# Three tile rings instead of one in the retention stage, and sums of squares over both heads of a pair at once

## The chip, the cores and the metric

The kernel runs on one core of a Trainium2 chip. The metric is the device time of one execution in microseconds (us). The core has a matrix engine (TensorE, PE in the profile; its weight loads are PEld), three engines for elementwise work (VectorE = DVE, ScalarE = ACT, GpSimd = POOL) and SyncE (SP), whose queue issues most of the DMA transfers. Each engine runs its own instructions strictly in order. An instruction that must wait holds up everything behind it on its engine.

## The reference, cut to what matters

One layer of a streaming encoder on a sequence of 2048 tokens, width 1024: a normalised input is projected to 7168 columns, which feed a chunked attention branch (8 heads), a retention branch (8 heads, key size 64, value size 128) and gates; the two branches are projected back, gated, merged, projected once more and normalised. The part that the change touches is the retention branch and its norm by head:

```python
s = jnp.einsum('bnqhd,bnkhd->bnhqk', qc, kc) * intra_decay
o_intra = jnp.einsum('bnhqk,bnkhe->bnqhe', s, vc)
...
state = state * chunk_decay[None, :, None, None] + kv_n        # from chunk to chunk
o_cross = jnp.einsum('bnqhd,nbhde->bnqhe', qc, state_prev) * cross_decay.T[:, :, None]
o = (o_intra + o_cross).astype(jnp.float32).reshape(B, S, H, dv)
mean = jnp.mean(o, axis=-1, keepdims=True)
var = jnp.mean(jnp.square(o - mean), axis=-1, keepdims=True)
o = (o - mean) * lax.rsqrt(var + GN_EPS)
o = o.reshape(B, S, H * dv) * gn_gain.astype(jnp.float32)
branch_r = jnp.einsum('bsf,fd->bsd', o_r * jax.nn.silu(g_r), w_out_ret[l])
```

## The kernel before, in words

Every float32 matrix operand is split into a high and a low part, and products are made of three matmuls (high by high, high by low, low by high). The large products ("dense work": jobs `p0`, `g0`, `p1`, `g1`, `ba`, `br`, `out`, tiles named `ps_...`, `wh_...`, `wl_...`) are one long stream of steps of three to six matmuls. The two halves of the sequence (s = 0 and 1) each go through an attention stage and a retention stage, and there the dense stream fills the time between the stage's own matmuls: `fill(n)` (L683) emits some n steps of it. Work that must come a little later is put off by a number of steps with `later` (L245), stores with `put` (L258). So the order on every engine is fixed in the program text; almost all of it is recorded through one helper, which is why nearly every row of the profile has line L143.

**Retention** (L1612) works on 16 units in each half: pairs of heads p = 0 to 3, and for each pair four steps `st` of 256 tokens. In unit (p, st) it does for each head i = 0, 1 of the pair:

- `scores`: four matmuls into a PSUM tile `sr`; then DVE multiplies by the decay mask (`sm <- sr, dm`, 128x384), ACT rounds that to its high part (`sh <- sm`), POOL makes the low part (`sl <- sm, sh`).
- `output`: matmuls into one half of the PSUM tile `o`, of which there is only one (`bufs=1`): first the state times q (`o <- qr, sstk`), then `sh` and `sl` with the values `vr`.

After the second head, `evacuate`: ACT copies `o` to `oz` (stored to DRAM as `ors`) and squares it to `o2`, then splits `o2` into `o2h` (ACT) and `o2l` (POOL). One unit later, `sums` lets PE add up the squares over the 128 value rows: a matmul with a one-hot column matrix `ohr` puts the sum into one row of the PSUM tile `ssq`. At the end of a stage a chain of 12 DVE operations makes 1/sqrt of it, which is stored as `rsscr`; much later `finish_yr` (L1237) loads a row of it, broadcast over the partitions, as `rb`.

Loads of a unit: `kr` (2 DMAs), `qr` for head 0 and head 1 (2 DMAs each), issued two units ahead; `kd` and two `vr`, issued one unit ahead; two masks `dm` for each pair. All of them go through SP's queue, together with the stores.

All of these tiles, loads, masks, scores, outputs and squares alike, come from **one ring** `E` of 22 buffers of 128x512 floats (2 KB a partition). The layer that builds the program gives a tile whichever buffer of its ring is free at that point of the order. The first instruction that writes the tile then waits until the buffer's previous tile has been read for the last time: by a matmul, by an elementwise operation, or, for a tile that is stored, until the store has landed.

Of the kernel before, what the change touches and what calls it, by code (L numbers as in the profile page):

```python
# [11 lines left out]
F32 = mybir.dt.float32  # L12
F32R = mybir.dt.float32r
# [8 lines left out]
P = 128  # L22
# [6 lines left out]
B = 512  # L29
NB = SEQ // B  # L30
T = 256
# [22 lines left out]
CS = 6  # L54
E_PROJ = 19
E_ATT = 11
E_RET = 22
E_MRG = 23
PR_BUFS = 5
ATT_FILLS = (1.0, 1.0)  # L60
# [9 lines left out]
ONE = 31  # L70
# [3 lines left out]
def hybrid_kernel(  # L74
# [28 lines left out]
    epool, xpool = [None], [None]  # L103
# [10 lines left out]
    def E(name, dt=F32, shape=(P, 512)):  # L114
        return epool[0].tile(list(shape), dt, tag="e", name=name)
# [37 lines left out]
    pe, act, dve, pool = Ordered(nc.tensor), Sometimes(nc.scalar), Sometimes(nc.vector), Sometimes(nc.gpsimd)  # L153
    dma = Ordered(nc.sync).dma_start
# [9 lines left out]
    ohr = const.tile([P, NOH], F32R, name="ohr")  # L164
# [1072 lines left out]
    def finish_yr(h, b, m, lead, hold=0):  # L1237

        a, u, r = (E(f"{n}_{h}_{b}") for n in ("yr", "yv", "rb"))
        dma(a, orscr[h // 2][b][h % 2])  # L1240
        dma(u, urscr[h][b])
        dma(r, rsscr[b // 2][8 * b + h].rearrange("(o d) -> o d", o=1).broadcast_to([P, B]))

        def gated():
            dve.scalar_tensor_tensor(a, a, gn[:, h:h + 1], u, ALU.mult, ALU.mult)

        later(lead, gated)
        later(lead + 2, lambda: (pool if m is None else dve).tensor_tensor(a, a, r, ALU.mult))
        if m is None:
            put(lead + 8, yrscr[h], a)  # L1250
            return
        wh, wl = (w[:, h % 4, :] for w in R[m])
        at = max(lead + 5, hold - steps[0])
        later(at, lambda: act.copy(wh, a))
        later(at + 2, lambda: dve.tensor_tensor(wl, a, r32(wh), ALU.subtract))
# [356 lines left out]
    def retention(s, ps_ret):  # L1612
# [43 lines left out]
        def load_state(p, st):  # L1656

            if st == 4:
# [2 lines left out]
                dma(r32(sstk).rearrange("p i c -> p (i c)"), r32(skscr[p]))  # L1661
                sstks[p, 4] = sstk

        def load_mask(p, i):
            dms.setdefault(p, []).append(E(f"dm_{p}_{i}")[:, 0:T + P])
            dma(dms[p][i], dmask[2 * p + i])

        def scores(p, st, i):

            nm = f"{p}_{st}_{i}"  # L1670
            ks, qs = tiles[p, st]
            sp = ps_ret.tile([P, 512], F32, tag="sr", bufs=2, name=f"sr_{nm}")[:, 0:T + P]
            for kk in range(2):
                o = sp[:, kk * T:T + kk * P]
                kcol = ks[:, i, kk * P:(kk + 1) * P]
                pe.matmul(o, kcol, qs[i][:, 0, kk * P:], start=True, stop=False)
                pe.matmul(o, kcol, qs[i][:, 1, kk * P:], start=False, stop=True)
            got = []

            def masked():  # L1680
                sm = E(f"sm_{nm}")[:, 0:T + P]
                dve.tensor_tensor(sm, sp, dms[p][i], ALU.mult)
                later(2, lambda: high(sm))

            def high(sm):
                got.append(E(f"sh_{nm}", F32R)[:, 0:T + P])
                act.copy(got[0], sm)
                later(2, lambda: low(sm))

            def low(sm):  # L1690
                got.append(E(f"sl_{nm}", F32R)[:, 0:T + P])
                pool.tensor_tensor(got[1], sm, r32(got[0]), ALU.subtract)

            later(1, masked)
            return got
# [63 lines left out]
        def evacuate(p, st, ops):  # L1759
            b, un = st // 2, st % 2  # L1760
            nm = f"{p}_{st}"
            got = []

            def out_():
                oz = E(f"oz_{nm}")
                o2 = E(f"o2_{nm}")
                act.copy(oz, ops)
                act.activation(o2, ops, AF.Square)
                put(
                    2,  # L1770
                    orscr[p][b][:, :, un * T:(un + 1) * T].rearrange("i p t -> p i t"),
                    oz.rearrange("p (i t) -> p i t", i=2),
                )
                later(2, lambda: high(o2))

            def high(o2):
                got.append(E(f"o2h_{nm}", F32R))
                act.copy(got[0], o2)
                later(2, lambda: low(o2))

            def low(o2):
                got.append(E(f"o2l_{nm}", F32R))
                pool.tensor_tensor(got[1], o2, r32(got[0]), ALU.subtract)

            later(1, out_)

            def sums():
                sure(lambda: len(got) == 2)
                for i in range(2):
                    r = 8 * b + 2 * p + i  # L1790
                    for n, t in enumerate(got):
                        pe.matmul(
                            ssq[:, un * T:(un + 1) * T], ohr[:, ONE - r:ONE - r + 32],
                            t[:, i * T:(i + 1) * T],
                            start=not begun[0], stop=(p == 3 and st == 4 * s + 3 and i == 1 and n == 1),
                            skip_group_check=True,
                        )
                        begun[0] = True

            return sums  # L1800

# [240 lines left out]
```

## Time and profile before

| | |
|---|---|
| Time, median of three runs | 1909.71 us (1906.38, 1909.71, 1910.21) |
| The profiled execution | 1909.69 us, of which its span, first to last instruction, is 1907.9 us |
| PE busy over the span | 1866.9 us (98%) |
| Retention of half 0 (566 to 735 us) | 169.0 us, PE busy 161.80 us, DMA engines 88% busy |
| Retention of half 1 (1313 to 1497 us) | 184.0 us, PE busy 180.40 us, DMA engines 91% busy |

In the quoted views, a row of the waits is "who waited <- for whom: us in total, times, longest us"; a row of the timeline is "start us, length us, engine, line, operation, out<-in, count, [idle time of the engine before it <- what ended it]"; a row of the windows is "from:to, length, busy us (x instructions) of PE, PEld, DVE, ACT, POOL, then granted TensorE clock, busy share of the DMA engines, GB/s". The median time of the three runs and the profiled execution agree to 0.02 us.

### The profile page before, as it was taken

The page shows a single profiled execution, that of the slowest core. Times are in us where ns is not written, and L with a number is a line of the kernel's source. Part 1 is how long each engine was busy: PE and PEld are TensorE (multiplying, and loading weights), DVE is VectorE, ACT ScalarE, POOL GpSimd, SP SyncE. Part 2 cuts the span into 40 slices and gives each one's busy share as a digit, 9 for nine tenths or more (in the row PEclk, how much of TensorE's full clock was granted, in tenths as well). Part 3 has the DMA queues.
Part 4 walks back from the last instruction along what each step waited for, and adds up shares of the span by engine and source line. Part 5 has one row for each costly group of instructions (what it writes and reads, how often), then busy time and mean ns, then how long its engine had stood idle before and what let it go on. Part 6 is the DMA issues. An engine that isn't in the chain of part 4 may idle for free. (4 is left out here: it accounts for less than half of the span.)

```text
span 1907.9 us, 31062 instructions
## 1 busy us (share of the span) xinstructions
PE 1866.9 (98%) x10213; PEld 1604.4 (84%) x10213; DVE 1355.7 (71%) x2456; ACT 933.1 (49%) x1931; POOL 665.3 (35%) x583
## 2 busy tenths in 40 slices
PE   7999999999999999999999999999999999999998
PEld 6899889888888888899889888887888878888886
DVE  6879888677655658889798677765546766767665
ACT  7555554666654455443333666664455321223544
POOL 0102105455645561001105554554564000002775
PEclk9999999999999999999999999999999999999999
DMA  6586976666549987775776656555998999986673
GB/s 197 158 275 200 282 265 213 185 193 185 175 144 278 279 257 258 231 233 195 222 247 202 185 165 180 166 150 155 275 283 265 326 355 345 322 291 227 209 238 127
DMA packets 325553, 435.88 MB, mean 228 GB/s; under 512 B 29880, under 2 KB 191184, under 8 KB 325392
## 3 DMA queue, kind: packets, MB, share of 16 engines
q1 hardware_dynamic: 260096, 368.35, 60.7%
q10 hardware_dynamic: 65296, 65.55, 11.2%
q8 instruction: 81, 1.33, 0.3%
q14 instruction: 80, 0.66, 0.1%
HBM read 288.14 MB, written 145.64 MB: 227 GB/s over the span
## 5 line engine op out<-in xcount | busy, mean ns | idle before, releaser
L143 POOL TENSOR_SCALAR pr<-pr,rsum 128x640 f32<-128x640 f32 (+4 forms) x128 | 100.0, 781 | 197.7 <-DVE rsum L143 130.7
L143 DVE TENSOR_TENSOR ptl<-tp,pth 128x512 fp32r<-128x512 f32 (+1 forms) x168 | 100.3, 597 | 91.7 <-ACT pth L143 77.8
L143 ACT ACTIVATE pr<-pr,mn 128x640 f32<-128x640 f32 (+4 forms) x128 | 97.9, 765 | 123.3 <-DVE mn L143 97.3
L143 PE MATMUL ps_g_x<-r,wh_g 128*128 128x512 f32 x448 | 141.5, 397 | 1.0 <-ACT u_g L143 0.9
L143 PE MATMUL ps_g_z<-r,wh_g 128*128 128x512 f32 x448 | 141.1, 396 | 0.0
L143 POOL TENSOR_TENSOR l_vr<-vrt,h_vr 128x512 fp32r<-128x512 f32 x32 | 47.7, 1492 | 202.4 <-DMA qrs<-l_q 131.6
L143 POOL TENSOR_TENSOR t_out<-raw_out 128x512 f32<-128x512 f32 x7 | 14.1, 2008 | 263.2 <-DVE wl_out L143 263.2
L143 DVE CUSTOM_DVE_ANT_0 pr<-wide,bt 128x640 f32<-128x640 f32 (+4 forms) x128 | 93.7, 732 | 16.5 <-PE wide L143 13.5
L143 ACT CAST pth<-tp 128x512 fp32r<-128x512 f32 (+1 forms) x168 | 85.3, 507 | 38.9 <-PE tp L143 34.2
L143 PE MATMUL wide<-ka,qa 128*128 128x384 f32 (+1 forms) x448 | 94.9, 327 | 2.9 <-DVE mn L143 2.7
L143 DVE TENSOR_TENSOR sm<-sr,dm 128x384 f32<-128x384 f32 x64 | 35.6, 556 | 85.3 <-PE sr L143 33.9
L143 ACT CAST wh_p<-raw_p 128x512 fp32r<-128x512 f32 x111 | 67.9, 618 | 51.0 <-PE ps_p_y L143 18.2
L143 POOL TENSOR_TENSOR sl<-sm,sh 128x384 fp32r<-128x384 f32 x64 | 69.8, 1090 | 64.8 <-ACT sh L143 44.0
L143 PEld LDWEIGHTS tp<-ident,pr 128*128 128x128 f32 x560 | 71.8, 141 | 23.5 <-POOL pr L143 1.0
L143 PEld LDWEIGHTS ps_g_x<-r,wh_g 128*128 128x128 f32 x448 | 79.6, 189 | 13.9 <-ACT u_g L143 2.3
L143 PEld LDWEIGHTS ps_g_z<-r,wh_g 128*128 128x128 f32 x448 | 79.5, 188 | 12.4
L143 PE MATMUL tp<-ident,pr 128*128 128x128 f32 x560 | 89.0, 272 | 0.3
L143 PE MATMUL ps_g_z<-r,wl_g 128*128 128x512 f32 x224 | 88.2, 394 | 0.0
L143 PE MATMUL ps_g_x<-r,wl_g 128*128 128x512 f32 x224 | 88.1, 393 | 0.0
L143 POOL TENSOR_TENSOR wl_g<-t_g,wh_g 128x512 fp32r<-128x512 f32 x56 | 75.5, 1349 | 35.1 <-ACT wh_g L143 33.8
L143 DVE TENSOR_TENSOR wl_p<-raw_p,wh_p 128x512 fp32r<-128x512 f32 x111 | 79.5, 723 | 7.7 <-ACT wh_p L143 5.4
L143 POOL TENSOR_TENSOR t_g<-raw_g,t_g 128x512 f32<-128x512 f32 x56 | 73.8, 1318 | 28.1 <-issue 8.9
(927 smaller groups left out, 6016.7 us busy)
## 6 DMA issues: line engine op xcount, KB each, us to landing
raw_g<-in_w_in_dram ACTq DMA_DIRECT2D x56, 512.0 KB, 4.9
raw_p<-in_w_in_dram ACTq DMA_DIRECT2D x50, 512.0 KB, 5.8
qa<-qas SPq DMA_DIRECT2D x128, 128.0 KB, 3.4
qr<-qrs SPq DMA_DIRECT2D x128, 128.0 KB, 4.8
vr<-vrs SPq DMA_DIRECT2D x64, 256.0 KB, 5.6
ka<-kas SPq DMA_DIRECT2D x56, 256.0 KB, 4.1
va<-vas SPq DMA_DIRECT2D x40, 256.0 KB, 3.4
kds<-kdt_k SPq DMA_DIRECT2D x32, 256.0 KB, 4.8
```

What stands on the lines that cost most here:

```text
L143: return tc.keep_in_program_order(op(*a, **k))
```

## The change

The ring of 22 becomes three rings, 11 buffers `e` of 2 KB for the loads (`kr`, `qr`, `kd`, `vr`) and the four tiles of the closing DVE chain, 9 buffers `d` of 1.5 KB for masks and scores (`dm`, `sm`, `sh`, `sl`, which only ever use 384 columns), and 4 buffers `o` of 2 KB for `oz`, `o2`, `o2h`, `o2l`. That is 24 buffers instead of 22 in 0.5 KB a partition less. The sums of squares of a unit are made by two matmuls over 512 columns (both heads at once) instead of four over 256. A unit then has one row of `ssq` (row 4 st + p, head and token along it) where it had two half rows, and the load of `rb` collects its row from two pieces of 256 floats.

```diff
-E_RET = 22
+E_RET = 11
+D_RET = 9
+O_RET = 4
...
         dma(a, orscr[h // 2][b][h % 2])
         dma(u, urscr[h][b])
-        dma(r, rsscr[b // 2][8 * b + h].rearrange("(o d) -> o d", o=1).broadcast_to([P, B]))
+        by_head = rsscr[b // 2].rearrange("(b u p) (i t) -> b p i u t", u=2, p=4, i=2)
+        dma(
+            r.rearrange("p (u t) -> p u t", u=2),
+            by_head[b, h // 2, h % 2].rearrange("(o u) t -> o u t", o=1).broadcast_to([P, 2, T]),
+        )
...
+        def D_(name, dt=F32):
+            return epool[0].tile([P, T + P], dt, tag="d", bufs=D_RET, name=name)
+
+        def O_(name, dt=F32):
+            return epool[0].tile([P, 512], dt, tag="o", bufs=O_RET, name=name)
+
         def load_mask(p, i):
-            dms.setdefault(p, []).append(E(f"dm_{p}_{i}")[:, 0:T + P])
+            dms.setdefault(p, []).append(D_(f"dm_{p}_{i}"))
             dma(dms[p][i], dmask[2 * p + i])
...
             def masked():
-                sm = E(f"sm_{nm}")[:, 0:T + P]
+                sm = D_(f"sm_{nm}")
...
-                got.append(E(f"sh_{nm}", F32R)[:, 0:T + P])
+                got.append(D_(f"sh_{nm}", F32R))
...
-                got.append(E(f"sl_{nm}", F32R)[:, 0:T + P])
+                got.append(D_(f"sl_{nm}", F32R))
...
             def out_():
-                oz = E(f"oz_{nm}")
-                o2 = E(f"o2_{nm}")
+                oz = O_(f"oz_{nm}")
+                o2 = O_(f"o2_{nm}")
...
-                got.append(E(f"o2h_{nm}", F32R))
+                got.append(O_(f"o2h_{nm}", F32R))
...
-                got.append(E(f"o2l_{nm}", F32R))
+                got.append(O_(f"o2l_{nm}", F32R))
...
             def sums():
                 sure(lambda: len(got) == 2)
-                for i in range(2):
-                    r = 8 * b + 2 * p + i
-                    for n, t in enumerate(got):
-                        pe.matmul(
-                            ssq[:, un * T:(un + 1) * T], ohr[:, ONE - r:ONE - r + 32],
-                            t[:, i * T:(i + 1) * T],
-                            start=not begun[0], stop=(p == 3 and st == 4 * s + 3 and i == 1 and n == 1),
-                            skip_group_check=True,
-                        )
-                        begun[0] = True
+                r = 4 * st + p
+                for n, t in enumerate(got):
+                    pe.matmul(
+                        ssq, ohr[:, ONE - r:ONE - r + 32], t, start=not begun[0],
+                        stop=(p == 3 and st == 4 * s + 3 and n == 1), skip_group_check=True,
+                    )
+                    begun[0] = True
```

No instruction changes its place on any engine; only the 64 matmuls fall away. What moves are the waits. In the rows below a tile's name is followed by its pair, its step, where it has one its head, and a running number; in brackets stands whom the instruction waits for (DMAHW... is the landing of a DMA).

On ACT, in the first retention stage around unit (3, 1), the rows before:

```order
L143 CAST sh_3_1_1_8790<-sm_3_1_1_8766 128x384 [waits DVE_49]
L143 ACTIVATE u2_g0_11_8410<-u2_g0_11_8410 128x512 [waits DVE_49]
L143 CAST wh_g0_12_2_8804<-t3_g0_12_8689 128x512 [waits PE_49]
L143 CAST sstk_3_1_8797<-state_7087 64x256 [waits DMAHW6_49]
L143 CAST sh_3_2_0_8847<-sm_3_2_0_8837 128x384 [waits DMAHW4_49,DVE_49]
L143 COPY u2_g0_12_8853<-ps_g0_12_x_8807 128x512 [waits PE_49]
L143 CAST wh_g0_12_4_8856<-t1_g0_12_8494 128x512
L143 COPY oz_3_1_8884<-o_3_1_8774 128x512 [waits PE_49,Pool_49]
L143 ACTIVATE o2_3_1_8885<-o_3_1_8774 128x512
```

and the same instructions in the changed kernel:

```order
L145 CAST sh_3_1_1_8766<-sm_3_1_1_8742 128x384 [waits DVE_49]
L145 ACTIVATE u2_g0_11_8392<-u2_g0_11_8392 128x512 [waits DVE_49]
L145 CAST wh_g0_12_2_8780<-t3_g0_12_8667 128x512 [waits PE_49]
L145 CAST sstk_3_1_8773<-state_7087 64x256 [waits DMAHW6_49]
L145 CAST sh_3_2_0_8823<-sm_3_2_0_8813 128x384 [waits DVE_49,Pool_49]
L145 COPY u2_g0_12_8829<-ps_g0_12_x_8783 128x512 [waits PE_49]
L145 CAST wh_g0_12_4_8832<-t1_g0_12_8476 128x512
L145 COPY oz_3_1_8858<-o_3_1_8750 128x512 [waits PE_49,Pool_49]
L145 ACTIVATE o2_3_1_8859<-o_3_1_8750 128x512 [waits DMAHW4_49]
```

The wait for a DMA has gone from `sh` of unit (3, 2), three instructions ahead of `oz` of unit (3, 1), to `o2` of unit (3, 1), behind `oz`.

On POOL, in the second retention stage, the low parts before:

```order
L143 TENSOR_TENSOR o2l_1_6_17060<-o2_1_6_16999,o2h_1_6_17021 128x512 [waits DVE_49,Activation_49]
L143 TENSOR_TENSOR sl_1_7_1_17062<-sm_1_7_1_17002,sh_1_7_1_17023 128x384 [waits DMAHW2_49,DMAHW3_49,PE_49,Activation_49]
L143 TENSOR_TENSOR t3_g1_12_17089<-raw_g1_12_0_16700,raw_g1_12_1_16751 128x512 [waits Pool_49]
L143 TENSOR_TENSOR sl_2_4_0_17095<-sm_2_4_0_17064,sh_2_4_0_17075 128x384 [waits Activation_49,Pool_49]
L143 TENSOR_TENSOR o2l_1_7_17188<-o2_1_7_17118,o2h_1_7_17144 128x512 [waits DMAHW6_49,DMAHW7_49,PE_49,Activation_49]
```

and in the changed kernel:

```order
L145 TENSOR_TENSOR o2l_1_6_17016<-o2_1_6_16955,o2h_1_6_16977 128x512 [waits PE_49,Activation_49]
L145 TENSOR_TENSOR sl_1_7_1_17018<-sm_1_7_1_16958,sh_1_7_1_16979 128x384 [waits Activation_49,Pool_49]
L145 TENSOR_TENSOR t3_g1_12_17045<-raw_g1_12_0_16662,raw_g1_12_1_16711 128x512
L145 TENSOR_TENSOR sl_2_4_0_17051<-sm_2_4_0_17020,sh_2_4_0_17031 128x384 [waits Activation_49,Pool_49]
L145 TENSOR_TENSOR o2l_1_7_17142<-o2_1_7_17072,o2h_1_7_17098 128x512 [waits PE_49,Activation_49]
```

The waits for landings of DMAs have left both kinds of low parts; `o2l` still waits for PE, which reads the buffer's previous tile.

## The prediction

> **What bounds the kernel now.** I read the page's first part, then the windows by stage, then who waits for whom on PE and on ACT in the two retention stages, then the timeline at the longest stall.
>
> ```profile
> PE 1866.9 (98%) x10213; PEld 1604.4 (84%) x10213; DVE 1355.7 (71%) x2456; ACT 933.1 (49%) x1931; POOL 665.3 (35%) x583
> ...
> 566.00:735.00 169.00, 161.80 (x933) 138.80 (x932) 93.83 (x181) 81.49 (x160) 95.67 (x79) 0.99 0.88 257
> 1313.00:1497.00 184.00, 180.40 (x1026) 155.06 (x1025) 98.24 (x182) 90.14 (x174) 94.11 (x77) 1.00 0.91 273
> ```
>
> PE is the bound: 98% busy. What a change of buffers can win is PE's idle time in the two retention stages, 169.00 - 161.80 = 7.2 us and 184.00 - 180.40 = 3.6 us, and what follows from it. The reader should also see the DMA engines at 0.88 and 0.91: they are the second limit of just these stages. Whom PE waits for there, the first stage's rows and then the second's:
>
> ```profile
> PE o L143 <- ACT o L143: 4.2, 4, 2.3
> PE sr L143 <- DMA qr<-qrs: 1.0, 2, 0.6
> PE kv L143 <- DMA vr<-vrs: 0.7, 1, 0.7
> ...
> PE ssq L143 <- POOL o2l L143: 0.5, 1, 0.5
> ...
> PE o L143 <- DMA sstk<-sks: 1.4, 1, 1.4
> PE o L143 <- ACT o L143: 1.4, 1, 1.4
> PE o L143 <- POOL sl L143: 0.4, 1, 0.4
> PE ssq L143 <- POOL o2l L143: 0.2, 1, 0.2
> ```
>
> Five times PE wants to write the one PSUM tile `o` and ACT has not yet emptied it. ACT is busy half of the time, so it must itself have waited; its own waits, in the two stages:
>
> ```profile
> ACT sh L143 <- DMA ors<-oz: 26.3, 6, 6.1
> ...
> ACT sh L143 <- DMA ors<-oz: 23.6, 8, 4.6
> ```
>
> That is a wait for a buffer: `sh` has nothing to do with the store of `oz`, it only got the ring's buffer from which that store was still reading. The longest case:
>
> ```profile
> 706.12 0.51 ACT L143 CAST sh<-sm 128x384 fp32r<-128x384 f32 x1 [6.09 <-DMA ors<-oz]
> ...
> 707.54 0.59 ACT L143 COPY oz<-o 128x512 f32<-128x512 f32 x1
> 708.01 0.61 ACT L143 ACTIVATE o<-o 128x512 f32<-128x512 f32 x1
> ...
> 706.02 0.40 PE L143 MATMUL ps_g_y<-r,wl_g 128*128 128x512 f32 x1
> 708.67 0.80 PE L143 MATMUL o<-qr,sstk 128*128 128x256 f32 x2 [2.25 <-ACT o L143]
> ...
> 708.00:713.00 5.00, 4.33 (x18) 4.07 (x19) 2.84 (x4) 2.99 (x7) 4.32 (x4) 0.66 0.80 232
> ```
>
> ACT stands 6.09 us before `sh`; behind it in its order stand `oz` and `o2` of the unit that PE has just finished; PE starts the next `o` 50 ns after `o2` ends. The last row shows the aftermath: the clock granted to TensorE in the next 5 us is 0.66.
>
> [...]
>
> **Waits of ACT that go.** From the addresses in the two built programs I took, for each tile of the stage, the tile that held its buffer before, and set the end of that one's last use against the start of the new one's first write, both by the trace of before. In the old ring 14 `sh` start right at the landing of an `ors` store. In the new one no `sh` follows `oz`: their buffers were read last by the score matmuls or by POOL, usually 7 us earlier; three `sh` of the first stage would wait 0.5 to 0.9 us for POOL. So the five waits of PE lose their cause, except one: at 660.10 PE waits after a late mask (the last row is DVE's idle time ahead of all `sm` that masks ended).
>
> ```profile
> 651.57 0.56 DVE L143 TENSOR_TENSOR sm<-sr,dm 128x384 f32<-128x384 f32 x1 [5.07 <-DMA dm<-in_dmask_dram]
> ...
> 660.10 0.50 PE L143 MATMUL o<-qr,sstk 128*128 128x256 f32 x2 [0.23 <-ACT o L143]
> ...
>   DMA dm<-in_dmask_dram: 18.9, 4
> ```
>
> The sum: 4.2 + 1.4 = 5.6 us idle. A matmul's shown end hides a little more: from 706.02 to 708.67 are 2.65 us where 0.23 is usual, 2.42 lost for 2.25 shown, so 0.17 for each of five, 0.85. The slow clock costs 5.00 x (1 - 0.66) = 1.7 us. Together 8.15. Off go 0.23 + 0.17 for 660.10 and a remainder at 708: `o2` there now waits for that same store itself, which landed at about 706.1; `o2` then ends at 706.7 at the earliest, against the 706.25 at which PE could go on, 0.5. **7.25 us** stay; bounds 0 (the new wait of `o2` replaces all, a rival below) and 8.15.
>
> **Waits of POOL that go.**
>
> ```profile
>   PE o L143: 15.6, 4
>   DMA kd<-kds: 4.8, 1
> ```
>
> These are POOL's idle times ahead of `o2l`: its buffer was still being read by the matmuls of a q, or a load that nobody reads had yet to land in it. In the ring of four it follows `o2l` of the unit before, free some 5 us earlier. PE's three waits for `o2l` and `sl` are 0.5 + 0.2 + 0.4 = **1.1 us**; bounds 0 and, with 0.17 for each, 1.6.
>
> **Sums of squares.**
>
> ```profile
> 589.26 0.62 PE L143 MATMUL ps_g_z<-r,wh_g 128*128 128x512 f32 x2
> 589.72 0.39 PE L143 MATMUL ps_g_z<-r,wl_g 128*128 128x512 f32 x1
> 589.94 0.28 PE L143 MATMUL ssq<-o2h,ohr 128*32 128x256 f32 x1
> ...
> 590.41 0.40 PE L143 MATMUL o<-qr,sstk 128*128 128x256 f32 x2
> ```
>
> Four matmuls over 256 columns take 590.41 - 589.94 = 0.47 us; two over 512 columns take the 0.46 us from 589.26 to 589.72. So halving the instructions wins 0.01 us in each of 32 units, **0.3 us**; bounds 0 and 0.6 (at 0.22 us, the step after 589.72). [...]
>
> **Loads in a ring of 11.** Two units hold 12 loads, and the loads of scores are issued two units ahead, so the q of the second head must wait until PE has used that of an earlier unit: by the comparison 5 times in the first stage (0.4 to 1.7 us later than before) and 11 times in the second (up to 3.1 us). In SP's order the second mask of a pair stands right behind. The case of unit (2, 5):
>
> ```profile
> 1403.59 3.21 SPq L143 DMA_DIRECT2D qr<-qrs  x4
> 1406.90 0.53 SPq L143 DMA_DIRECT2D dm<-in_dmask_dram  x1
> ...
> 1408.32 0.40 PE L143 MATMUL o<-qr,sstk 128*128 128x256 f32 x2
> 1418.44 0.62 PE L143 MATMUL sr<-qr,kr 128*128 128x256 f32 x4
> ...
> 1410.83 0.56 DVE L143 TENSOR_TENSOR sm<-sr,dm 128x384 f32<-128x384 f32 x1 [2.85 <-DMA dm<-in_dmask_dram]
> ...
> qr<-qrs SPq DMA_DIRECT2D x64, 128.0 KB, 4.3
> ```
>
> The third and fourth of these `qr` issues now wait for the `o` matmuls that start at 1408.32. Issued from 1408.7 on and landing 4.3 us later, by about 1413.6, they still come 4.8 us before the scores that read them at 1418.44: no cost while the landing takes under 9 us. The mask, issued near 1409.9 instead of 1406.90, makes DVE wait 2.85 + 3.0 = 5.9 us. The nearest row is 651.57: a wait of 5.07 us cost PE 0.4 in the end. Two masks in the second stage are hit so: **-0.7 us**, bounds 0 and 2 x 3.0 = 6.
>
> **The row in two pieces.** Queue rates show what twice the packets cost the 32 loads of `rb`:
>
> ```profile
> q1 hardware_dynamic: 260096, 368.35, 60.7%
> q10 hardware_dynamic: 65296, 65.55, 11.2%
> ```
>
> 71 ns for packets of 1416 B on average and 52 ns for 1004 B: about 0.046 ns a byte and 7 ns a packet. 128 more packets of 7 ns over 16 engines land a load 0.06 us later; the consumers run steps ahead of PE. Nothing; without that cover 32 x 0.06 = 2 us.
>
> **Crowding.** If the first stage loses some 6 us of 169, the same bytes raise the DMA share from 0.88 to 0.91, what the second stage already has. PE's waits for loads in the first, 1.0 + 0.7 us, may grow: **-0.6 us**, a third of them; bounds 0 and 1.7.
>
> Sum: 7.25 + 1.1 + 0.3 - 0.7 - 0.6 = 7.35 us. The profiled execution took 1909.69 us (span 1907.9 and 1.8 around it), the median is 1909.71, so **1902.3 us**.
>
> **Rivals.**
>
> 1. *The store catches ACT again, one tile further.* With four buffers `o2` (or `oz`) of a unit takes the buffer of the previous unit's `oz`, and must wait until that has landed.
>
> ```profile
> DMA to landing us min/median/max: 2.3/5.6/7.7
> ```
>
> These are the landings of the `oz` stores; SP issues some only 4 to 5 us after the copy, so that the whole can take the 10.6 us of a unit (169 / 16). By the comparison the landing leaves `o2` 0.4 to 3 us in most units, and in two it is late by 0.1 and 1.4 us, ahead of 1.7 to 2.5 us that ACT has in hand before PE. If denser traffic makes landings 2 us longer, most of the first stage's gain (4.2 + 0.7 + 1.7) is lost: about 7.35 - 5.5 = 1.9 us gained, 1907.8 us. For it: DMA at 0.88. Against it: the waits start later in ACT's order, where nothing but `o2` hangs on them.
> 2. *The ring of 11 becomes the bound* (slower). From a landing of 9 us on, the late q reach PE late. The longest landing in the rows above is 7.7 us, so it takes another 1.3 us; if then 11 + 5 units each lose 1 us and the masks 2, 18 - 7.35 = 10.6 us slower: 1920 us; half of that is 1915.
> 3. *More is won.* Masks that waited for `oz` buffers come sooner, SP no longer stands behind late `oz`, and the load waits of 1.0 + 0.7 + 1.4 us my two costs and the remainder at 708 go too: 7.35 + 3.1 + 1.3 + 0.5 = 12.3 us, 1897.4 us.
> 4. *Nothing changes,* because other waits in the same order replace each removed one: 1909.4 us with the 0.3 of the sums. Against it: ACT's idle time of 50 us hangs on one cause.
>
> **How the numbers follow.** Forecast (1899 to 1905) 0.60, rival 3 0.12, rival 1 0.16, rival 4 0.06, rival 2 0.06. The range for 8 in 10 runs from 1895.5 (a little below rival 3) to 1908.5 (rival 1 and a little). A measurement of this kernel can tell 0.2%, 3.8 us, from no change: faster has the forecast, rival 3 and a little of rival 1, 0.75; same 0.19; slower 0.06.
>
> **What would show it.** Right: in the changed profile ACT's row `sh <- DMA ors<-oz` is gone from both stages, PE's `o <- ACT o` falls from 5.6 us to under 1.5, PE's idle time from 7.2 and 3.6 us to about 3 and 2, and the granted clock stays 1.00 at the place of 708; the two `ssq` rows of 512 columns take as long as four. Rival 1 shows as ACT `oz` or `o` waiting for `ors<-oz`; rival 2 as PE `sr` waiting for `qr<-qrs` in the second stage; late masks as DVE `sm` waiting over 18.9 us in all. Wrong would be PE idle as before in these windows, or a loss outside them.

## The result, and the profile after

The changed kernel takes 1916.49 us (median of 12 executions, 1911.03 to 1921.08), the kernel before, on the same chip, 1909.95 us (12 executions, 1904.38 to 1914.12). The ratio is 1.0038 (95% interval 1.0028 to 1.0048): slower by 6.5 us, where 7.4 us faster was predicted. The profiled execution of the changed kernel took 1917.57 us, with a span of 1915.8 us.

The windows by stage, first of the changed kernel (the two retention stages, the stretch of the output projections behind them, and three short windows at stalls):

```profile
566.00:735.00 169.00, 165.68 (x923) 139.29 (x923) 102.05 (x187) 84.25 (x163) 97.25 (x80) 1.00 0.89 267
1313.00:1497.00 184.00, 179.25 (x977) 151.91 (x977) 100.20 (x182) 90.99 (x173) 90.01 (x75) 0.98 0.93 275
1497.00:1690.00 193.00, 185.75 (x797) 150.68 (x796) 128.60 (x199) 43.22 (x72) 0.00 (x0) 0.98 0.95 313
708.00:713.00 5.00, 3.77 (x23) 3.11 (x23) 0.56 (x2) 2.52 (x5) 4.32 (x4) 1.00 0.32 113
1465.00:1472.00 7.00, 6.17 (x22) 5.33 (x22) 2.96 (x8) 1.43 (x4) 2.25 (x2) 0.52 0.86 213
1526.00:1530.00 4.00, 2.74 (x7) 2.12 (x8) 2.71 (x5) 1.14 (x2) 0.00 (x0) 0.59 0.99 309
```

and of the kernel before, the stretch that the prediction did not look at:

```profile
1497.00:1690.00 193.00, 191.68 (x840) 156.95 (x840) 136.97 (x213) 45.62 (x76) 0.00 (x0) 1.00 0.95 333
```

PE's idle time in the first retention stage fell from 7.2 to 3.3 us and the clock at the place of 708 is whole, as forecast. In the second stage it rose from 3.6 to 4.75 us. The great loss lies behind both: in 1497 to 1690, idle time went from 1.3 to 7.25 us, and PE got through 797 matmuls where it had been 840. Whom PE waits for in the changed kernel, in the three stretches:

```profile
PE ssq L145 <- POOL o2l L145: 1.4, 2, 1.0
PE sr L145 <- DMA qr<-qrs: 0.7, 2, 0.4
...
PE o L145 <- POOL sl L145: 0.4, 2, 0.2
PE kv L145 <- DMA vr<-vrs: 0.2, 1, 0.2
...
PE kv L145 <- DMA vr<-vrs: 3.7, 3, 2.4
PE o L145 <- DMA sstk<-sks: 1.0, 1, 1.0
...
PE ps_ba_(0, 0)_18393 L145 <- ACT wh_ba_(0, 0)_18313 L301: 3.1, 1, 3.1
PE ps_ba_(0, 0)_18684 L145 <- ACT wh_ba_(0, 0)_18608 L301: 2.1, 1, 2.1
PE ps_ba_(0, 0)_18592 L145 <- ACT wh_ba_(0, 0)_18518 L301: 1.2, 1, 1.2
```

The row `o <- ACT o` is gone from both stages. New are `kv <- vr` in the second (3.7 us) and `ps_ba <- wh_ba` behind it. Putting the start of the same PE instruction in the two profiles side by side (the matmuls of `ssq` left out) shows the course: the changed kernel is 5.1 us ahead at 735 us, 6.7 us ahead at 1455, 2.1 us ahead at 1497, and 7.7 us behind at 1690, where it stays. So this execution was ahead by most of the predicted gain at 1455, and then 4.6 and 9.8 us were lost. Most of that lead is not the change's doing, however: the profiles of seven kernels that keep the ring of 22 (below) are 3.0 to 5.6 us ahead of the same profile at 1455.

Behind 1497 PE's idle time grew by 5.9 us, and two spells of half clock, 3.41 us each, at 1526.7 and 1567.7 us, cost by estimate some 1.7 us each (half of 3.41): together about 9 of the 9.8 us.

The last 9.8 us begin with one load. The same place in both kernels, with the issues of SP ahead; before:

```profile
1516.11 0.32 SPq L143 DMA_DIRECT2D rb<-rss  x1
...
1518.75 0.38 SPq L143 DMA_DIRECT2D raw_ba<-in_w_out_attn_dram  x1
...
1524.81 0.62 ACT L299 CAST wh_ba_(0, 0)_18377<-raw_ba 128x512 fp32r<-128x512 f32 x1 [1.86 <-DMA raw_ba<-in_w_out_attn_dram]
```

and after:

```profile
1515.93 0.37 SPq L145 DMA_DIRECT2D rb<-rss  x1
...
1518.57 0.38 SPq L145 DMA_DIRECT2D raw_ba<-in_w_out_attn_dram  x1
...
1523.21 0.69 DVE L1254 TENSOR_TENSOR yr<-yr,rb 128x512 f32<-128x512 f32 x1 [1.86 <-DMA rb<-rss]
...
1526.59 0.62 ACT L301 CAST wh_ba_(0, 0)_18313<-raw_ba 128x512 fp32r<-128x512 f32 x1 [2.02 <-DMA raw_ba<-in_w_out_attn_dram]
...
1523.77 0.39 PE L145 MATMUL ps_ba_(1, 1)_18365<-r,wl_ba_(1, 0)_18264 128*128 128x512 f32 x1
1527.26 1.22 PE L145 MATMUL ps_ba_(0, 0)_18393<-r,wh_ba_(0, 0)_18313 128*128 128x512 f32 x2 [3.10 <-ACT wh_ba_(0, 0)_18313 L301]
```

Both loads are issued 0.18 us earlier than before, yet the cast of `raw_ba`, whose data comes through the same queue behind `rb`, starts 1.78 us later: 8.0 us after its issue, not 6.1. PE stands 3.10 us, and the granted clock of the next stretch is 0.59. The rows that show `rb` in the two kernels, its landings and who waits for it (DVE, and SP, which stood 14 times before and 18 times after ahead of a later issue until an `rb` had landed; its row is for 1497 to 1665 us); before:

```profile
DMA to landing us min/median/max: 4.7/5.7/8.4
...
DVE yr L1248 <- DMA rb<-rss: 1.8, 3, 1.2
...
SPq L143 <- DMA rb<-rss: 5.4, 14, 0.8
```

and after:

```profile
DMA to landing us min/median/max: 5.6/7.3/8.6
...
DVE yr L1254 <- DMA rb<-rss: 18.7, 13, 4.4
...
SPq L145 <- DMA rb<-rss: 16.0, 18, 1.5
```

The 4.6 us ahead of 1497 are one stall, `kv` of unit (3, 6):

```profile
1462.54 0.40 PE L145 MATMUL ps_g_w<-r,wl_g 128*128 128x512 f32 x1
...
1465.29 0.55 PE L145 MATMUL kv<-vr,kd 128*128 128x256 f32 x1 [2.35 <-DMA vr<-vrs]
...
1466.38 1.01 PE L145 MATMUL kv<-vr,kd 128*128 128x256 f32 x3 [0.54 <-DMA vr<-vrs]
```

2.35 + 0.54 us of waiting, and the clock of 0.52 over 7 us in the windows above, which by estimate is 7 x (1 - 0.52) = 3.4 us more; the 1.4 us that the old kernel waits for ACT a little later are not lost here. That makes some 4.9 us, against the 4.6.

### The profile page after: what moved, and what is told of

It is laid out like the page before. It is cut to its first block, busy times and chain, and to the rows that moved or that the text cites. A ratio compares the mean times of both kernels' runs of the same rounds, so it can differ in the third digit from the quotient of the medians.

```text
span 1915.8 us, 30857 instructions
## 1 busy us (share of the span) xinstructions
PE 1871.8 (98%) x10149; PEld 1602.1 (84%) x10149; DVE 1362.8 (71%) x2456; ACT 935.2 (49%) x1931; POOL 662.8 (35%) x583
## 4 chain that ended last, share of the span: by engine, by line
PE 61%; DMA 9%; DVE 3%; issue 2%; ACT 2%; SPq 1%; POOL 0%; DVEq 0%; ACTq 0%; POOLq 0%
PE ps_g_z L145 6%; PE ps_g_x L145 5%; PE ps_p_x L145 4%; PE ps_p_z L145 4%; PE ps_g_v L145 3%; PE ps_g_w L145 3%; PE po L145 3%; PE ps_g_y L145 3%; PE ps_out_z L145 2%; PE o L145 2%; PE ps_out_x L145 2%; PE wide L145 2%; PE ps_p_y L145 2%; PE ps_p_v L145 2%; PE tp L145 2%
## 5 line engine op out<-in xcount | busy, mean ns | idle before, releaser
L145 DVE CUSTOM_DVE_ANT_0 pr<-wide,bt 128x640 f32<-128x640 f32 (+4 forms) x128 | 93.7, 732 | 16.5 <-PE wide L145 13.5
```

The source lines that it names most:

```text
L145: return tc.keep_in_program_order(op(*a, **k))
```

## The experiments

Theory P: the loss is that of `rb` in two pieces. Rival G: the gained time is given back because loads bound the stretch from 1455 us. Rival R: the ring of 11 loads makes SP late. All runs were timed against the kernel before on the same chip. The table gives the median, the ratio to before with its 95% interval, and how much longer than in the profile of before the stretch from 1497 to 1690 is (starts of the same two PE instructions).

| run | rings (loads, scores, outputs) | sums | `rb` | median us | ratio | stretch us |
|---|---|---|---|---|---|---|
| the change | 11, 9, 4 | new | two pieces | 1916.49 | 1.0038 (1.0028 to 1.0048) | +9.8 |
| e1_rings | 11, 9, 4 | old | whole | 1905.87 | 0.9987 (0.9974 to 1.0000) | -0.9 |
| e2_sums | one of 22 | new | two pieces | 1917.15 | 1.0047 (1.0029 to 1.0065) | +11.8 |
| e3_whole | 11, 9, 4 | new, four stores | whole | 1912.39 | 1.0017 (1.0008 to 1.0027) | +1.7 |
| e4_pieces | one of 22 | old, four stores | two pieces | 1923.09 | 1.0070 (1.0056 to 1.0084) | +14.8 |
| e5_one_store | 11, 9, 4 | new | whole | 1907.43 | 0.9988 (0.9974 to 1.0001) | -0.6 |
| e6_four | one of 22 | old | four pieces | 1923.72 | 1.0076 (1.0058 to 1.0093) | +15.2 |
| e7_two | one of 22 | old | two pieces | 1920.72 | 1.0060 (1.0040 to 1.0079) | +10.4 |
| e8_ring12 | 12, 8, 4 | new | whole | 1901.37 | 0.9962 (0.9948 to 0.9977) | -0.7 |
| e9_spare | one of 22 | old | whole, and a spare load | 1910.52 | 1.0002 (0.9989 to 1.0016) | +1.8 |
| e10_ring13 | 13, 7, 4 | new | whole | 1905.72 | 0.9979 (0.9966 to 0.9992) | -0.5 |
| e11_d8 | 11, 8, 4 | new | whole | 1909.64 | 1.0009 (0.9995 to 1.0023) | +0.2 |
| e12_rb_first | 11, 9, 4 | new | two pieces, first | 1932.85 | 1.0122 (1.0101 to 1.0144) | +22.9 |
| e13_two_loads | 11, 9, 4 | new | two loads | 1922.17 | 1.0078 (1.0063 to 1.0092) | +13.5 |
| e14_own_rows | one of 22 | old | two pieces, own rows | 1906.50 | 0.9995 (0.9983 to 1.0006) | -1.2 |
| e15_pieces12 | 12, 8, 4 | new | two pieces | 1913.19 | 1.0037 (1.0018 to 1.0055) | +10.2 |
| e16_sums_alone | one of 22 | new | whole | 1908.93 | 1.0006 (0.9994 to 1.0018) | +0.1 |
| e17_rings12 | 12, 8, 4 | old | whole | 1904.26 | 0.9972 (0.9958 to 0.9987) | -0.5 |

### The parts of the change, one by one

**e1_rings**: the three rings alone.

```diff
-E_RET = 22
+E_RET = 11
+D_RET = 9
+O_RET = 4
```

> The changed kernel with the sums of squares and the load of rb as before: the three rings alone. Theory P (the pieces): the time lost behind 1455 us comes from rb in two pieces, whose landing grew from 5.7 to 7.3 us and for which DVE then waits up to 4.4 us ahead of yr; without it the gain of 6.7 us stays: 1903 us, the ps_ba rows of PE wait for wh_ba by under 2 us in all, no half clock at 1526 and 1567. Theory G (given back): the out-projection stretch from 1455 us is bound by loads, and PE only comes too early for them: the time is lost whatever rb does, 1910 to 1916 us, and the stall of kv for vr at 1465 stays. Theory R (the ring of 11 holds up SP, so that the vr of unit (3, 6) comes late): that stall of 3.5 us stays alone, about 1906 us.

Measured 1905.87 us. The stretch behind 1497 is as before: `yr` waits 2.3 us for `rb`, and PE for a single `wh_ba`:

```profile
DVE yr L1250 <- DMA rb<-rss: 2.3, 2, 2.0
...
PE ps_ba_(0, 0)_18748 L145 <- ACT wh_ba_(0, 0)_18672 L301: 1.0, 1, 1.0
```

That is theory P for the loss, and against G, by which the loss would have stayed. R's 1906 us fits the time, but the stall that R leaves is not there: `kv` of unit (3, 6) waits 0.33 and 0.20 us, and PE waits 2.25 us for a `qr` at 597 us instead. Of the gain of 6.7 us only 2.5 us (by the ratio, whose interval reaches 1.0000) to 4 us (by the medians) is there, which P does not explain.

**e2_sums**: the ring of 22 kept; new sums, `rb` in two pieces.

> The kernel before with the sums of squares over both heads and the load of rb in two pieces, its one ring of 22 kept. Theory P: slower by what the pieces cost, 7 + 6.7 = up to 13 us, at least 5: 1915 to 1923 us, with DVE's yr waiting for rb by over 10 us. Theories G and R: nothing, 1909.5 us, since PE comes no earlier and the ring is the old one.

Measured 1917.15 us, `yr` waits 21.8 us for `rb`. P again; G and R said nothing would happen.

**e3_whole** and **e4_pieces** should split the sums from the pieces by rearranging the 32 rows in the store. In e3_whole (e4_pieces does the reverse to the old rows):

```diff
-        chain.append(lambda: dma(rsscr[s], y))
+        def store():
+            for b in (2 * s, 2 * s + 1):
+                for u in range(2):
+                    r = 8 * b + 4 * u
+                    dma(rsscr[s][8 * b:8 * b + 8, u * T:(u + 1) * T].rearrange("(p i) t -> p i t", i=2),
+                        y[r:r + 4].rearrange("p (i t) -> p i t", i=2))
+        chain.append(store)
```

> The changed kernel with rb loaded as one piece of 2 KB a partition: the sums of squares stay as changed, and the 32 rows are put into the old order by the store (four stores for one, each 4 partitions). Theory P: as e1_rings, 1903 us, rb lands in 5.7 us again and the waits of yr for rb fall from 14 us to 2. Theory G: 1910 to 1916 us. Theory R: 1906 us.

> The kernel before, its ring and its sums of squares kept; the store of the 32 rows writes them in the changed order, so that rb is loaded in two pieces of 1 KB a partition. Theory P: as e2_sums, 1915 to 1923 us. Theories G and R: 1909.5 us. If e2_sums is slow and this one is not, the matmuls of the sums of squares cost it.

e4_pieces (1923.09 us, at the upper end of P's range) speaks for P, though its four stores are new too. e3_whole fits no theory whole. Its time, 1912.39 us, lies in G's range, and the stall of `kv` near 1465 that G and R keep is there (2.41 and 0.89 us, at 1470), but the stretch behind 1497 loses only 1.7 us, as P has it. So either the sums cost something, or the four stores did.

**e5_one_store** makes one store of it, by another row number, so that a head's 512 floats come to lie together:

```diff
-                r = 4 * st + p
+                r = 8 * b + 2 * p + un
...
-        chain.append(lambda: dma(rsscr[s], y))
+        by_row = rsscr[s].rearrange("(i r) (u t) -> (r u) i t", i=2, u=2)
+        chain.append(lambda: dma(by_row, y.rearrange("r (i t) -> r i t", i=2)))
...
-        by_head = ...                  # two pieces
+        dma(r, rsscr[b // 2][16 * (h % 2) + 4 * b + h // 2].rearrange("(o d) -> o d", o=1).broadcast_to([P, B]))
```

> The changed kernel with rb whole and a single store: the row of ssq is 8b + 2p + un, and the store writes both heads' halves so that a head's 512 floats lie together. Rings and 512 wide sums of squares are the change's own. Theory P2 (pieces cost about 7 us, the four stores of e3_whole about 6, the sums about nothing): as e1_rings, 1903 to 1907 us. Rival S (the 512 wide sums of squares are what made e3_whole 6 us slower than e1_rings): about 1912 us.

Measured 1907.43 us, ratio 0.9988: as e1_rings, and not S's 1912 us. The sums cost nothing that can be measured. **e16_sums_alone**, the same three edits with the ring of 22:

> The kernel before, its one ring of 22 kept, with the sums of squares over both heads, rb whole and the single store of e5_one_store: the sums alone. The prediction's term: 0.3 us faster, so 1909.3 us and no difference that can be measured. If the sums or the store cost something of their own: 1912 us or more.

Measured 1908.93 us, ratio 1.0006 (0.9994 to 1.0018): nothing that can be measured. Against e5_one_store the four stores of e3_whole cost it some 5 us; but e11_d8 below, also with 11 loads and one store, is at 1.0009 (0.9995 to 1.0023), which is not told apart from e3_whole. The profile of e3_whole has the longest waits for q and values of all runs (8.1 us), which lie ahead of the second store, so that one profile does not show where the four stores act. What made e3_whole slow stays open.

### What it is in the pieces that costs

**e7_two** changes nothing but the load (its halves are other heads'), **e6_four** makes four pieces of 512 B:

```diff
-        dma(r, rsscr[b // 2][8 * b + h].rearrange("(o d) -> o d", o=1).broadcast_to([P, B]))
+        by_head = rsscr[b // 2].rearrange("(b u p) (i t) -> b p i u t", u=4, p=2, i=4)
+        dma(r.rearrange("p (u t) -> p u t", u=4),
+            by_head[b, h % 2, h // 2].rearrange("(o u) t -> o u t", o=1).broadcast_to([P, 4, P]))
```

> The kernel before with only the load of rb changed to two pieces of 1 KB a partition; store and sums of squares are as before, so that the halves come from rows of other heads (their scales are wrong). Theory P2: rb lands in 7.3 us, DVE's yr waits about 20 us for it, 1916 to 1918 us. Rival Y (the loss in e2_sums comes from the store or the sums in their new order): 1909 to 1911 us.

> The kernel before with rb loaded in four pieces of 512 B a partition, taken from rows of other heads (so part of the scales of the outputs are wrong). Theory P2, by packets: rb landed in 5.7 us with one piece and 7.3 with two; another 256 packets add 3.2 us, 10.5 us landing, and DVE's yr waits for rb in nearly all 24 loads; slower than e7_two by 6 us or more, 1923 us and above. Rival Y (the order of the rows, or the place of the halves in memory, makes the load late): as e7_two.

e7_two takes 1920.72 us, slower even than P2's 1916 to 1918 and far from Y's 1909 to 1911: the load alone does it. For e6_four the size was wrong: `rb` lands in the same time with four pieces as with two, and the kernel is 3 us slower than e7_two, not 6 or more. The landings of e7_two, then of e6_four:

```profile
DMA to landing us min/median/max: 5.9/7.1/8.6
```

```profile
DMA to landing us min/median/max: 5.6/7.3/8.7
```

So the cost does not go by the number of packets. **e9_spare** adds as many packets to before as two pieces do, but from 128 places and into a tile that nobody reads:

```diff
+        if m is not None:
+            spare = epool[0].tile([P, 256], F32, tag="spare", bufs=1, name=f"sp_{h}_{b}")
+            dma(spare, dmask[0][:, 0:256])
```

> The kernel before with one more load in each of the 24 fillings of the output projections: 128 packets of 1 KB into a tile that nobody reads, right behind rb, which stays whole. Theory T (throughput: in the stretch from 1497 to 1665 us the 16 DMA engines are 0.96 busy, and what the pieces add there is engine time): 24 x 128 x 48 ns over 16 engines is 9 us more engine time; the pieces added about 24 x 0.54 = 13 us and cost 7 to 11 us, so 5 to 8 us slower, 1914 to 1918 us. Theory L (lateness: rb itself comes 1.6 us later, and DVE's order waits for it): rb lands as before, yr waits for rb by about 2 us, and the time is within 2 us of before.

Measured 1910.52 us, ratio 1.0002 (0.9989 to 1.0016). Theory T falls: the DMA engines rise to 0.99 and 350 GB/s, and PE goes on.

```profile
1497.00:1665.00 168.00, 165.40 (x723) 134.68 (x722) 118.09 (x180) 38.74 (x64) 0.00 (x0) 1.00 0.99 350
```

**e12_rb_first** puts the load of `rb` ahead of those of `yr` and `yv`:

> The changed kernel with the load of rb (in its two pieces) issued ahead of those of yr and yv in place of behind them, about 1 us earlier. Theory L: yr's waits for rb fall from 18.7 us to under 8, and about half of the 7 to 11 us come back: 1909 to 1913 us. Theory T: the same packets pass through the same engines, 1914 to 1919 us, the waits only move to yr <- yv.

Measured 1932.85 us, 16 us slower than the change, which both theories missed. The waits for `rb` are gone, as L has it, and have moved to `yv`, as T has it; but `yv`, now queued behind `rb`, is needed two steps sooner, and the waits have grown. This fits lateness, not throughput, as the cost; and what counts is not `rb` itself but whatever DVE needs first behind it:

```profile
DVE yr L1251 <- DMA yv<-urs: 47.4, 24, 5.9
```

**e13_two_loads** issues the halves as two loads, **e14_own_rows** lets each partition read two pieces of its own (of the stored output, in place of the scales):

```diff
+        for half in range(2):                                          # e13_two_loads
+            dma(r[:, half * T:(half + 1) * T],
+                by_head[b, h // 2, h % 2, half:half + 1].broadcast_to([P, T]))
...
+        dma(r.rearrange("p (u t) -> p u t", u=2),                      # e14_own_rows
+            orscr[h // 2][b][:, :, 0:T].rearrange("u p t -> p u t"))
```

> The changed kernel with the two pieces of rb loaded by two loads of 128 KB, each of 128 packets of 1 KB from one row, in place of one load of 256 packets. Theory F (form: one load whose 128 partitions share one source in several pieces holds the queue; a single piece does not): each half lands 0.35 us after the load ahead of it, as the spare loads of e9_spare did, and the loss of the pieces is gone: 1906 to 1909 us. Theory K (many small packets from one address): each half holds the queue for about 1 us, and the time stays at 1914 to 1919 us.

> The kernel before with rb loaded in two pieces of 1 KB a partition of which each partition reads its own (from the stored output, so the scales of the outputs are wrong): as many packets as in e7_two, in the same order, but from 128 places. If the shared source makes the pieces slow: rb lands some 0.7 us after the load ahead of it, in 5.7 us, yr waits for it by about 2 us, 1908 to 1912 us. If two pieces a partition are slow from anywhere: as e7_two, 1917 to 1922 us.

e13_two_loads takes 1922.17 us: theory K, and 3 us above its range. e14_own_rows takes 1906.50 us, ratio 0.9995: no loss. Their rows of `rb`, first of e13_two_loads:

```profile
DMA to landing us min/median/max: 4.7/6.3/7.5
...
DVE yr L1255 <- DMA rb<-rss: 26.3, 19, 3.2
```

and of e14_own_rows:

```profile
DMA to landing us min/median/max: 3.8/5.3/7.8
```

How much later than the load ahead of it a load lands can be worked out from issues and landings: the time from the landing of the load issued just ahead to its own, where that one landed over 1.5 us after its issue. Medians over 10 to 20 loads between 1497 and 1670 us:

| load | size | us behind the load ahead |
|---|---|---|
| `yv`, each partition its own 2 KB (before) | 256 KB | 0.65 |
| `rb` whole, 2 KB shared by all (before; e1, e5, e8) | 256 KB | 0.69; 0.65 to 0.66 |
| `rb` in two pieces of 1 KB, shared (the change; e2; e7) | 256 KB | 2.04; 2.11; 1.83 |
| `rb` in four pieces of 512 B, shared (e6) | 256 KB | 2.13 |
| one piece of 1 KB, shared (e13) | 128 KB | 1.08 |
| two pieces of 1 KB, each partition its own (e14) | 256 KB | 0.68 |
| one piece of 1 KB, each partition its own (e9) | 128 KB | 0.35 |

What costs in these runs is a piece of 1 KB or 512 B that all partitions read (1.08 to 2.13 us a load). Neither the packets of 1 KB (0.35 us in e9_spare) nor the form of two pieces (0.68 us in e14_own_rows) does it alone.

These are delays of landings, not rates of the DMA engines. For the two loads shown above, issued at 1516.11 and 1515.93 us, the windows from the landing of `yv` to that of `rb` are, before and after:

```profile
1520.68:1521.34 0.66, 0.66 (x5) 0.54 (x4) 0.52 (x1) 0.00 (x0) 0.00 (x0) 1.00 1.04 400
1520.47:1523.12 2.65, 2.65 (x14) 2.18 (x13) 0.75 (x2) 0.00 (x0) 0.00 (x0) 1.00 0.95 289
```

In the 2.65 us the engines are 0.95 busy and move some 770 KB, of which `rb` is 256 KB: they go on with other loads. The trace has 16 completions for each load. For the `rb` loads between 1497 and 1665 us, the first comes 3.97 us (median) after the issue in both kernels, the last 5.71 us before and 7.31 us after. Most packets of 1 KB take 46 ns in both kernels, but the slowest in twenty take at least 54 ns before, 153 ns in the change, 128 ns in e7_two and 53 ns in e14_own_rows. So a few packets take long, and the landing in the views is the last of the 16 completions (5.7 us before, 7.3 us after); that it is these packets it waits for is the author's inference. Why they take long is not shown.

The medians hide a scatter. Four of the 15 loads of the change land within 0.70 us, like a whole row. Of the 15 whole rows of before, seven take 0.93 to 2.28 us, while of the 15 loads of e14_own_rows only one takes over 0.71 us. So a whole row that all partitions read is late at times too, though not often enough to show in the time (e14_own_rows, whose interval holds 1).

### What the rings gave

**e8_ring12** is e5_one_store with 12 loads and 8 scores, **e10_ring13** with 13 and 7, **e11_d8** with 11 and 8, **e15_pieces12** is the change with 12 and 8, **e17_rings12** is e1_rings with 12 and 8:

```diff
-E_RET = 11
-D_RET = 9
+E_RET = 12
+D_RET = 8
```

> e5_one_store with a ring of 12 loads in place of 11 and of 8 masks and scores in place of 9. Theory Q (part of the rings' gain goes to q that wait in the ring of 11: 2.4 us at 597 us in the profile of e1_rings): PE's waits sr <- qr are under 1 us, and it is 1 to 3 us faster than e5_one_store. Rival D (eight masks and scores are too few, sh waits for POOL or PE): slower than e5_one_store by 1 to 5 us.

> e8_ring12 with 13 loads and 7 masks and scores. Theory Q (the ring of 11 held up SP; 12 suffice for two units): within 2 us of e8_ring12, 1900 to 1903 us. Rival D (masks and scores become the scarce buffers at 7): slower than e8_ring12 by 2 us or more, with sh or sm waiting for POOL or PE.

> e5_one_store with 8 masks and scores in place of 9, its ring of 11 loads kept. Theory Q: the gain of e8_ring12 over e5_one_store came from the twelfth load alone, so this is no faster than e5_one_store: 1906 to 1909 us, with PE's waits kv <- vr and sr <- qr of 4 to 6 us together. Rival: the smaller ring of masks made it, 1901 to 1903 us.

> The changed kernel, rb in its pieces, with 12 loads and 8 masks and scores in place of 11 and 9. If ring and pieces add up: faster than the changed kernel by the 5 to 6 us between e5_one_store and e8_ring12, 1909 to 1912 us, with no wait of kv for vr over 1 us near 1465. If the pieces alone decide what follows 1455 us: 1914 to 1918 us.

> The kernel before with the three rings alone, in the sizes 12, 8 and 4: e1_rings with a twelfth load. Theory Q (the twelfth load makes the difference between e1_rings and e8_ring12, the sums nothing): as e8_ring12, 1900 to 1903 us, ratio to before 0.995 to 0.998, waits of kv for vr and sr for qr of about 2 us together in the two retention stages, against 3.6 to 8.1 in the runs with 11. Rival: e8_ring12 was a lucky set of runs, or its sums and its store in rows of both heads were part of it: as e1_rings, 1904 to 1908 us.

e8_ring12 takes 1901.37 us, 6.1 less than e5_one_store (Q had 1 to 3), and is the fastest of all; e11_d8, with 8 scores but 11 loads, gains nothing (1909.64). So between these kernels the gain hangs on the twelfth load, as theory Q has it. e17_rings12 (1904.26) and e10_ring13 (1905.72) are faster than before too, beyond their intervals, but by less, and Q's 1900 to 1903 us was missed by both (e17_rings12, whose ratio lies in Q's range, still waits 4.0 us for q and values, where Q said 2); e17_rings12 against e1_rings, 1.6 us, is not resolved. With 13 loads rival D's sign is there: `sm` waits 16.9 us for POOL's `sl` over the two stages, against 3.1 us in e8_ring12; 7 masks and scores are too few. e15_pieces12 gains 3.3 us on the change by the medians and nothing by the ratios (1.0037 and 1.0038): there, rings and pieces do not add up. PE's waits in the second retention stage, in e5_one_store and then in e8_ring12, show what the twelfth load changes:

```profile
PE kv L145 <- DMA vr<-vrs: 2.6, 3, 1.6
PE o L145 <- DMA sstk<-sks: 1.4, 1, 1.4
```

```profile
PE o L145 <- DMA sstk<-sks: 1.3, 1, 1.3
PE kv L145 <- DMA vr<-vrs: 0.4, 1, 0.4
```

Over all profiles, PE's idle time in the two retention stages (the rows added up), mean and in brackets the least and the most:

| | `o <- ACT o` | `kv <- vr` and `sr <- qr` | `ssq <- o2l` |
|---|---|---|---|
| one ring of 22 (before and seven runs) | 4.5 (3.0 to 5.6) | 2.0 (1.1 to 3.8) | 0.4 to 0.7 |
| 11 loads (the change and six runs) | 0.2 (0 to 1.0) | 5.3 (3.6 to 8.1) | 1.4 to 1.6 |
| 12 or 13 loads (four runs) | 1.1 (0 to 2.3) | 2.3 (1.1 to 4.0) | 1.4 to 1.6 |

With 11 loads, 4.3 us of waits for ACT go and 3.3 + 0.9 us of waits for loads and POOL come: all of PE's waits in the two stages together are 9.7 us (mean) with the ring of 22, 9.6 us with 11 loads and 7.8 us with 12 or 13. The stall of `kv` of unit (3, 6) is 1.7 to 3.3 us in six of the seven profiles with 11 loads, and at most 0.6 us in the four with 12 or 13; with the ring of 22 it is at most 1.2 us but for e4_pieces (2.0).

## Why the prediction was wrong

- **The row in two pieces** is the step that failed: it was given nothing, with 2 us if the cover were gone, and costs 10.6 us (1916.49 of the change less 1905.87 of e1_rings) or 9.7 us by their ratios; e7_two alone, 11. Its price of 0.06 us a load came from the packets of whole queues; the load lands 1.4 us later behind the one ahead of it (2.04 us in the median, against 0.65 to 0.69). No row of before showed small pieces of one row read by all partitions, so it should have had a wide bound. And "the consumers run steps ahead of PE" looked only at `rb`'s own consumers: behind it in the queue stand `raw_ba`, `yr`, `yv` and `ga`, and PE waited for `wh_ba`. The prediction's test "a loss outside them" is what came.
- **Waits of ACT that go**: the mechanism was right, `sh <- ors` is gone from both stages, and `o <- ACT o` went from 5.6 us to 0. The size was not. It was summed from one execution, which was the worst of eight with the old ring: the others have 3.0 to 5.2 us there. The half clock behind 708, 1.7 us of the sum, appears in only one of the seven others near that place. In those seven the stretch from 566 to 735 us, with the same ring as before, is 2.3 to 4.7 us (mean 3.4) shorter than in the profile of before; with 11 loads it is 0.9 to 5.0 us shorter (mean 2.8). The 5.0 us that the changed kernel shows there are therefore mostly not the change's doing.
- **Waits of POOL that go** did not: `ssq <- o2l` and `o <- sl` were 1.1 us and are 1.8 us. The long wait is new and the same in every kernel with the ring of four outputs.
- **Sums of squares**: 0.3 us forecast, nothing to be measured (e16_sums_alone). In the traces the four matmuls take 0.469 us and the two 0.467 us (medians of 30 units), which is under 0.1 us in 32 units; that two rows of 512 columns take as long as four of 256 holds.
- **Loads in a ring of 11**: priced at 0.7 us for late masks, and indeed `sm` waits 35.3 us for masks where it was 18.9. But the price is paid elsewhere: PE waits 3.3 us more for q and values. It is the second rival's mechanism at a fifth of its size (16 us for late q), and its worst place in the changed kernel was `vr`, which stands behind q in SP's order, and not a q. That a held q made this `vr` late is argued from the order; that a twelfth load takes the stall away is what the runs show.
- **Crowding**: the DMA share of the first stage rose to 0.89, not 0.91, and the waits for loads there did not grow (1.7 us before, 0.9 after), so this term was not seen.
- The first rival is there, but small: ACT now waits for the store at `o2` (shown as `o`), as said, and in the changed kernel PE does not; in the other kernels with three rings PE's waits for ACT at `o` reach 2.3 us (table above). The rows of the change, first stage and second:

```profile
ACT o L145 <- DMA ors<-oz: 4.0, 4, 1.4
...
ACT o L145 <- DMA ors<-oz: 0.6, 1, 0.6
```

Of the 13.9 us between forecast and result, some 10 are the pieces. The rest is the rings, which were to win 7.05 us and won 2.5 to 4 us in e1_rings; the intervals of e1_rings, e5_one_store and e11_d8 all reach 1, so that a gain from rings with 11 loads is not shown.

## What to carry to other kernels

Price a load by who shares its source and by everything that is queued behind it, not by its bytes and its own consumer: the same 256 KB as two pieces a partition took the kernel to 1920.72 us from a shared source (e7_two) and to 1906.50 us from rows of their own (e14_own_rows). A changed access pattern that no row of the trace shows is an unknown, however small its data. Waits that depend on landings differed from one profile to the next (`o <- ACT o` with the old ring from 3.0 to 5.6 us): a gain summed from the worst stalls of one profile is an upper end, so look at a second execution, or take less. When a shared ring is split, give the part for the loads what the order of the issues keeps in flight: here 12 for two units (1901.37 us in e8_ring12), and 11 gave most of the gain back (1907.43 us in e5_one_store).

## What was not expected of the hardware

- A load of 256 KB in pieces of 512 B or 1 KB that 128 partitions read from one place landed 1.8 to 2.1 us after the load ahead of it, and the same row as one piece of 2 KB mostly 0.65 to 0.69 us, like rows of their own (table above). The DMA engines stayed busy meanwhile (0.95 in the 2.65 us windowed above); a few packets took long (the slowest in twenty of 1 KB at least 153 ns in the change, 54 ns before). Why 2 KB mostly escapes was not tried.
- 24 more loads of 128 KB into a stretch where the DMA engines are 0.96 busy cost nothing that can be measured (e9_spare, ratio 0.9989 to 1.0016): a busy share of 0.99 was not a bound there, while later landings of single loads (e7_two) cost 11 us.
- The granted clock was 0.50 for a few us beside some waits of PE and not beside others. In the profile of before it was so for 3.41 us from 278.6 and from 708.7 us, beside waits of 1.46 us (at 277) and 2.25 us (at 708); in that of the change for 3.41 us from 277.4, 1526.7 and 1567.7 us, beside waits of 1.74, 3.10 and 2.13 us, and for 6.83 us from 1465.3 us, beside one of 2.35 us. None follows the wait of 2.25 us at 597 in e1_rings, nor those of 1.44 us at 1335 and 1.40 us at 1473 before, and in the retention stages a wait was followed so in four of eight profiles with the old ring and four of seven with 11 loads. What decides it is not shown.
